# Stick-breaking weights by summation by parts: values replaced by their steps, running products used as they are

## The chip, the cores and the metric

The kernel runs on one core of a Trainium2 chip. The metric is the device time of one execution in microseconds; times below are the median of several executions, and every duration comes from one profiled execution.

## The reference, cut to what matters

The program is a trunk of two layers over 1024 tokens of width 1024. The first layer mixes tokens with two groups of attention heads, eight heads of width 64 each; the second mixes them with a recurrence; each layer ends with a feed-forward block. The change lies in the second head group of the first layer, stick-breaking attention:

```
z = einsum('bqhd,bkhd->bhqk', q_blk, k) * scale
causal = kpos[None, :] < qpos[:, None]
log_beta = log_sigmoid(z)
log_1m_beta = where(causal, log_sigmoid(-z), 0.0)
after = cumsum(log_1m_beta, axis=3, reverse=True) - log_1m_beta
w = where(causal, exp(log_beta + after), 0.0)
out = einsum('bhqk,bkhd->bqhd', w, v)
```

So for a query q the weight of key k is sigmoid(z_k) times the product of sigmoid(-z_j) over the keys j between k and q. Call C_k the product of sigmoid(-z_j) over all j from k up to the query, with C = 1 at the query and behind it. Then w_k = C_(k+1) - C_k, a difference of neighbouring running products.

## The kernel before, in words

**Tiling.** Heads are worked in pairs p. Pairs 4 to 7 are the stick-breaking heads, pairs 0 to 3 the softmax heads; the sequence is 4, 5, 6, 7, 0, 1, 2, 3. For each pair `project` makes queries and keys: four groups (queries and keys, each for two halves of the tokens) of 24 TensorE matmuls of 128x512 (lines 166 to 168) into PSUM tile `psq`, of which there are two buffers. ScalarE and VectorE take every group out of PSUM (lines 326 to 335) before its buffer can be used again. Values are made for two pairs at once by `v_tile` (lines 291 to 293) and taken out by `evacuate` (lines 303 to 306) into tiles `v`, 128 partitions by 8 token blocks by 128 columns: token 128t + p lies in partition p, block t.

**Weights.** Each weight block (128x1024 fp32, 512 KB) is loaded by a DMA that SyncE (SP) issues into a tile `raw`, of which there are three buffers, and is split into a rounded high part (`whi`, line 155, ScalarE) and the rest (`wlo`, line 156, VectorE). When both have read it, the `raw` buffer is free.

**Attention.** `attend` takes blocks of 128 queries, i = 0 to 7. For a stick-breaking head TensorE makes scores `sc` (lines 389, 390), ScalarE takes the sigmoid into `pr` (line 397), GpSimd (POOL) sets ones at and above the diagonal (line 408) and one column to the right (line 407), VectorE runs a scan from right to left (line 411) that leaves the running products C, and then subtracts neighbours (line 415) for the weights. TensorE turns 128x128 blocks of them (line 427), ScalarE copies these out of PSUM (line 431), and TensorE multiplies them with the values (line 356). Value products are held back until i = 3, 5, 6 and 7 and then run in one burst.

**What sets the order.** The program is written pair after pair, but a scheduler with a timeline of its own then orders the instructions of each engine before the program is built; it also decides which buffer a tile gets. Every engine, and the DMA queue of SyncE too, works in that order: an instruction that waits holds up all behind it on its engine. Matmuls of the next projection are thus mixed with the attention of the pair before.

Of the kernel before, what the change touches and what calls it, by code (L numbers as in the profile page):

```python
# [8 lines left out]
F32 = mybir.dt.float32  # L9
F32R = mybir.dt.float32r  # L10
BF16 = mybir.dt.bfloat16
AF = mybir.ActivationFunctionType
ALU = mybir.AluOpType
PSUM = bass.MemoryType.PSUM

P = 128
S = 1024
# [3 lines left out]
NT = S // P  # L21
# [78 lines left out]
class Trunk:  # L100
# [164 lines left out]
    def attention(self, x_src, xT_src, w_v, w_qk, bias_t, o_dst, hT, pools, open_first):  # L265
        nc, tc = self.nc, self.tc
        with ExitStack() as ctx:
# [6 lines left out]
            def turned_bank():  # L274
                return self.pt.tile([P, 512], F32, tag="tr", bufs=2, name=self.uid("tr"))
# [22 lines left out]
            def evacuate(vt, t2, both=False):  # L298
                psv = psvs.pop(t2)
                for tt in range(2):  # L300
# [4 lines left out]
                        nc.scalar.activation(vt[0][:, t, :], psv[:, tt, 0, :], AF.Copy, scale=rsc[:, t:t + 1])  # L305
                    nc.scalar.activation(vt[1][:, t, :], psv[:, tt, 1, :], AF.Copy, scale=rsc[:, t:t + 1])

            def v_alloc():
                return [ap.tile([P, NT, P], F32, tag="v", bufs=3, name=self.uid("v")) for _ in range(2)]

            def project(p, ws=(None, None)):
                st = [[ap.tile([P, S], F32R, tag="st", bufs=12, name=self.uid("st"))
                       for _ in range(3)] for _ in range(2)]
                for which in range(2):
                    w = ws[which] or self.split(w_qk[p, which], KT, P)
                    for half in range(2):
                        ps = prp.tile([P, 512], F32, tag="proj", bufs=2, name=self.uid("psq"))
                        self.proj_T(ps, w, slice(0, P), hT, half)
                        cs = slice(half * HALF, (half + 1) * HALF)
                        if which or p < 4:  # L320
                            nc.vector.tensor_tensor(ps, ps, rsb[:, cs], op=ALU.mult)
                        for h in range(2):
                            own, oth = (slice(0, 64), slice(64, P)) if h == 0 else (slice(64, P), slice(0, 64))
                            qs, k1, k2 = st[h]
                            if which == 0:
                                nc.scalar.activation(qs[own, cs], ps[own, :], AF.Copy, scale=-0.125)
                                nc.vector.scalar_tensor_tensor(
                                    qs[oth, cs], ps[own, :], -0.125, qs[own, cs].bitcast(F32),
                                    op0=ALU.mult, op1=ALU.subtract)
                            else:  # L330
                                nc.scalar.copy(k1[own, cs], ps[own, :])
                                nc.scalar.copy(k1[oth, cs], ps[own, :])
                                nc.vector.tensor_tensor(k2[own, cs], ps[own, :], k1[own, cs].bitcast(F32),
                                                        op=ALU.subtract)
                                nc.vector.tensor_copy(k2[oth, cs], k2[own, cs].bitcast(F32))
                return st

            def attend(p, st, vt):
                bias = [None, None]
# [25 lines left out]
                for i in range(NT):  # L365
                    k0 = max(0, i - 4) if p < 4 else 0
                    nb = i + 1 - k0
                    n = nb * P
# [4 lines left out]
                    w = n // n_c  # L373
                    for h in range(2):
                        qs, k1, k2 = st[h]
                        q = qs[:, i * P:(i + 1) * P]
                        if p < 4 and h == 1:
                            pr = ap.tile([P, 640], F32, tag="nata", bufs=3, name=self.uid("pr"))
                        else:
                            pr = ap.tile([P, 1024], F32, tag="nat", bufs=4, name=self.uid("pr"))  # L380
                        if p < 4:
                            mn = ap.tile([P, 2], F32, tag="mn", bufs=4, name=self.uid("mn"))
                            mn = [mn[:, c:c + 1] for c in range(n_c)]
                            sm = ap.tile([P, 1], F32, tag="sm", bufs=4, name=self.uid("sm"))
                        for c in range(n_c):
                            sc = pp.tile([P, 512], F32, tag="sc", bufs=3, name=self.uid("sc"))[:, :w]
                            ks = slice(k0 * P + c * w, k0 * P + c * w + w)
                            cs = slice(c * w, c * w + w)
                            nc.tensor.matmul(sc, q, k1[:, ks], start=True, stop=False)
                            scored = nc.tensor.matmul(sc, q, k2[:, ks], start=False, stop=True).ins  # L390
                            if p < 4:
                                off = 640 - n + c * w
                                nc.vector.tensor_tensor_reduce(
                                    pr[:, cs], sc, bias[h][:, off:off + w], 1.0, 3e38,
                                    op0=ALU.add, op1=ALU.min, accum_out=mn[c])
                            else:
                                nc.scalar.activation(pr[:, cs], sc, AF.Sigmoid, scale=rsc[:, i:i + 1])
                        if p < 4:
                            if n_c == 2:
                                nc.vector.tensor_tensor(mn[0], mn[0], mn[1], op=ALU.min)  # L400
                            nc.scalar.activation(pr[:, :n], pr[:, :n], AF.Exp, bias=mn[0], scale=-1.0,
                                                 accum_out=sm)
                            nc.vector.reciprocal(sm, sm)
                            nc.gpsimd.tensor_scalar(pr[:, :n], pr[:, :n], sm, 1.0, op0=ALU.mult, op1=ALU.mult)
                        else:
                            if n < S:
                                nc.gpsimd.memset(pr[:, n:n + 1], 1.0)
                            nc.gpsimd.affine_select(pr[:, n - P:n], pr[:, n - P:n], pattern=[[-1, P]],  # L408
                                                    compare_op=ALU.is_gt, fill=1.0, base=0,
                                                    channel_multiplier=1)  # L410
                            nc.vector.tensor_tensor_scan(  # L411
                                pr[:, 0:n][:, ::-1], pr[:, 0:n][:, ::-1], self.zero.to_broadcast([P, n]),
                                1.0, op0=ALU.mult, op1=ALU.add)
                            m = n if n < S else n - 1
                            nc.vector.tensor_tensor(pr[:, 0:m], pr[:, 1:m + 1], pr[:, 0:m], op=ALU.subtract)
                            if m < n:
                                nc.vector.memset(pr[:, m:n], 0.0)
                        nat.append(pr)
                    if p == seq[-1]:
                        self.scored.append(scored)  # L420
# [1 line left out]
                    for b0 in range(0, len(blocks), 4):  # L422
                        bl = blocks[b0:b0 + 4]
                        tr = turned_bank()
                        pt = ap.tile([P, 512], F32, tag="pt", bufs=7, name=self.uid("pt"))
                        for j, (kb, h) in enumerate(bl):
                            turned = nc.tensor.transpose(tr[:, j * P:(j + 1) * P],  # L427
                                                         nat[h][:, kb * P:(kb + 1) * P], self.ident).ins
                        w = len(bl) * P
                        if p >= 4 or (b0 // 4) % 2 == 0:  # L430
                            nc.scalar.copy(pt[:, :w], tr[:, :w])
                        else:
                            nc.vector.tensor_copy(pt[:, :w], tr[:, :w])
                        groups.append((i, nb, k0, bl, pt))
                        if not stretch:
                            values(groups, [])
                            groups = []
# [9 lines left out]
            vt = v_alloc()  # L447
# [89 lines left out]
            wk = self.split(None, KT, P, raw=wk)  # L537
            spread(1)
            st = project(seq[0], (wq, wk))
            for j, p in enumerate(seq):  # L540
                if j == 7:
                    prj.close()
                    pools[0] = open_first()
                attend(p, st, vt)
                if j < 7:
                    q = seq[j + 1]
                    if q % 2 == 0:
                        wv = v_weights(q // 2)
                        vt = v_alloc()
                        for t2 in range(4):  # L550
                            v_tile(q // 2, wv, vt, t2)
                            evacuate(vt, t2, q < 4)
                    st = project(q)


    def psum(self):
# [695 lines left out]
```

## Time and profile before

| | |
|---|---|
| time, median of 3 | 2198.3 us (2197.07 to 2202.79) |
| profiled execution, its own time | 2198.43 us |
| span from first to last instruction | 2196.6 us |
| TensorE busy | 2161.5 us, 98% |
| VectorE busy | 1540.9 us, 70% |
| ScalarE busy | 1171.1 us, 53% |
| GpSimd busy | 217.7 us, 10% |
| stick-breaking pairs 4 to 7 | from about 35 to about 303 us of the span |

Busy time of TensorE is the union of matmuls whose ends are modelled, so a share of 98% doesn't mean that no time is lost. In the rows, PE is TensorE, DVE VectorE, ACT ScalarE, POOL GpSimd and SPq the DMA queue of SyncE; L415 is line 415 of the program. Only some 270 us of the span hold what the change touches; the rest is feed-forward, recurrence and softmax attention.

### The profile page before, as it was taken

The numbers are of one execution on the slowest core, as the hardware profiler recorded it, in microseconds if no ns is written. First come the engines' busy times: TensorE is split into PE (matmuls) and PEld (weight loads), VectorE is DVE, ScalarE is ACT, GpSimd is POOL, SyncE is SP. The second block draws the span as 40 slices with busy tenths as digits, with TensorE's granted clock in tenths as the row PEclk, the third lists the DMA queues.
The fourth block names the chain that finished last, engine by engine and source line by source line (L and its number), as shares of the span: only waits on it lengthen the run. The fifth ranks groups of instructions, "written<-read, shape, count | busy, mean of one in ns | idle before, by whom it ended". The sixth has DMA issues, their size and how long they took to land.

```text
span 2196.6 us, 30590 instructions
## 1 busy us (share of the span) xinstructions
PE 2161.5 (98%) x11140; PEld 1803.2 (82%) x11140; DVE 1540.9 (70%) x2526; ACT 1171.1 (53%) x2174; POOL 217.7 (10%) x450
## 2 busy tenths in 40 slices
PE   9999999999999999999999999999999999999998
PEld 8888889878788888888887777888788888888886
DVE  5877865656878777776767677437787777758675
ACT  6655555556755444443446676528754444424443
POOL 2111113121100000000001333102000000000011
PEclk9999999999999999999999999999999999999999
DMA  7101011126323333336468411356233333328565
GB/s 273 34 30 49 27 37 49 54 84 221 137 91 111 117 98 115 94 123 230 144 183 253 130 58 39 100 192 221 86 120 106 101 112 99 115 87 287 172 182 155
DMA packets 168279, 270.21 MB, mean 123 GB/s; under 512 B 13889, under 2 KB 94785, under 8 KB 168129
## 3 DMA queue, kind: packets, MB, share of 16 engines
q1 hardware_dynamic: 167488, 266.18, 37.8%
q10 hardware_dynamic: 640, 2.10, 0.3%
q8 instruction: 87, 1.43, 0.3%
q14 instruction: 64, 0.52, 0.1%
HBM read 202.69 MB, written 65.54 MB: 122 GB/s over the span
## 4 chain that ended last, share of the span: by engine, by line
PE 87%; DVE 5%; DMA 3%; ACT 3%; issue 2%; POOL 0%; SPq 0%; POOLq 0%; ACTq 0%; DVEq 0%
PE ps L742 12%; PE ps L744 12%; PE ps L743 12%; PE ps L585 8%; PE ps L827 5%; PE ps L829 5%; PE ps L828 5%; PE tr L427 3%; PE pso L356 3%; PE psq L166 2%; PE psq L167 2%; PE psq L168 2%; PE ps L166 2%; PE ps L167 2%; PE ps L168 2%
## 5 line engine op out<-in xcount | busy, mean ns | idle before, releaser
L742 PE MATMUL ps<-hS,q 128*128 128x512 f32 (+1 forms) x1288 | 490.2, 381 | 0.7 <-ACT hS L96 0.4
L743 PE MATMUL ps<-hS,q 128*128 128x512 f32 (+1 forms) x1288 | 489.6, 380 | 0.9 <-DVE hS L89 0.9
L744 PE MATMUL ps<-hS,q 128*128 128x512 f32 (+1 forms) x1288 | 489.0, 380 | 0.0
L713 DVE TENSOR_TENSOR q<-raw,q 128x512 fp32r<-128x512 f32 x308 | 204.5, 685 | 181.6 <-ACT q L712 181.0
L743 PEld LDWEIGHTS ps<-hS,q 128*128 128x128 f32 x1288 | 242.7, 188 | 47.7 <-DVE hS L89 1.3
L742 PEld LDWEIGHTS ps<-hS,q 128*128 128x128 f32 x1288 | 242.3, 188 | 47.3 <-ACT hS L96 0.8
L744 PEld LDWEIGHTS ps<-hS,q 128*128 128x128 f32 x1288 | 242.7, 188 | 45.9
L712 ACT CAST q<-raw 128x512 fp32r<-128x512 f32 x308 | 177.7, 616 | 162.5 <-DVE raw L721 129.4
L828 PE MATMUL ps<-o,o 128*128 128x512 f32 x616 | 240.0, 390 | 0.5 <-DVE o L823 0.5
L829 PE MATMUL ps<-o,o 128*128 128x512 f32 x616 | 238.0, 390 | 0.5 <-DVE o L957 0.5
L700 ACT ACTIVATE raw<-raw,gcol 128x256 f32<-128x256 f32 x352 | 150.3, 498 | 143.3 <-DMA raw<-in_ffn_w_up_dram 71.6
L827 PE MATMUL ps<-o,o 128*128 128x512 f32 x616 | 221.4, 391 | 3.3 <-ACT o L956 3.0
L822 ACT CAST o<-raw 128x512 fp32r<-128x512 f32 x184 | 110.8, 621 | 160.3 <-PE ps L829 59.1
L182 POOL TENSOR_SCALAR rs<-ss 128x1 f32<-128x1 f32 x52 | 24.6, 473 | 1423.6 <-ACT junk L178 1356.9
L823 DVE TENSOR_TENSOR o<-raw,o 128x512 fp32r<-128x512 f32 x184 | 123.1, 686 | 56.1 <-ACT o L822 55.3
L827 PEld LDWEIGHTS ps<-o,o 128*128 128x128 f32 x616 | 115.5, 188 | 30.2 <-ACT o L956 4.8
L828 PEld LDWEIGHTS ps<-o,o 128*128 128x128 f32 x616 | 115.6, 188 | 25.3 <-DVE o L823 1.5
L829 PEld LDWEIGHTS ps<-o,o 128*128 128x128 f32 x616 | 115.6, 188 | 25.1 <-DVE o L957 1.4
L156 DVE TENSOR_TENSOR wlo<-raw,whi 128x1024 fp32r<-128x1024 f32 x76 | 93.4, 1228 | 58.5 <-ACT whi L155 57.8
L411 DVE TENSOR_TENSOR_SCAN pr<-pr,zero 128x128 f32<-128x128 f32 (+7 forms) x64 | 86.8, 1360 | 30.7 <-POOL pr L408 25.7
L155 ACT CAST whi<-raw 128x1024 fp32r<-128x1024 f32 x76 | 79.7, 1050 | 50.2 <-PE ps L167 19.9
L166 PE MATMUL psq<-hT,whi 128*128 128x512 f32 x256 | 101.8, 397 | 0.1
(206 smaller groups left out, 4314.2 us busy)
## 6 DMA issues: line engine op xcount, KB each, us to landing
raw<-in_ffn_w_gate_dram SPq DMA_DIRECT2D x44, 512.0 KB, 4.2
raw<-in_ffn_w_up_dram SPq DMA_DIRECT2D x44, 512.0 KB, 4.2
gS<-c SPq DMA_DIRECT2D x88, 256.0 KB, 3.6
raw<-gS SPq DMA_DIRECT2D x88, 256.0 KB, 2.8
gA<-c SPq DMA_DIRECT2D x66, 256.0 KB, 3.4
raw<-in_ffn_w_down_dram SPq DMA_DIRECT2D x63, 256.0 KB, 4.4
raw<-gA SPq DMA_DIRECT2D x44, 256.0 KB, 2.8
t<-in_ffn_w_down_dram SPq DMA_DIRECT2D x22, 512.0 KB, 6.8
```

Source lines behind the costliest of these rows:

```text
L166: nc.tensor.matmul(ps, wh[:, kt, cols], hh[:, kt, :], start=kt == 0, stop=False)
L585: self.matmul = nc.tensor.matmul(ps[:, n * 512:(n + 1) * 512], x, y[:, n, :], start=first and i == 0, stop=last and i == len(passes) - 1).ins
L700: nc.scalar.activation(raw[:, i], raw[:, i], AF.Copy, scale=gain[:, 4 * k + i:4 * k + i + 1])
L712: self.last = nc.scalar.copy(t[:, 0], src).ins
L713: self.last_lo = nc.vector.tensor_tensor(t[:, 1], src, t[:, 0].bitcast(F32), op=ALU.subtract).ins
L742: nc.tensor.matmul(ps, a[:, 0, kt, :], bh, start=kt == 0, stop=False)
L743: nc.tensor.matmul(ps, a[:, 0, kt, :], bl, start=False, stop=False)
L744: self.matmul = nc.tensor.matmul(ps, a[:, 1, kt, :], bh, start=False, stop=kt == 3).ins
L823: tt(t[:, 1], src, t[:, 0].bitcast(F32), op=ALU.subtract)
L827: nc.tensor.matmul(ps, a[0], b[:, 0], start=first, stop=False)
L828: nc.tensor.matmul(ps, a[0], b[:, 1], start=False, stop=False)
L829: nc.tensor.matmul(ps, a[1], b[:, 0], start=False, stop=last)
```

## The change

The sum of (C_(k+1) - C_k) v_k over the keys is rewritten by parts: it equals the sum of (1 - C_k) (v_k - v_(k-1)), with v before the first token taken as 0. So the differences move from the weights, which are made for every query, to the values, which are made once.

- The subtraction of neighbours on VectorE, the memset of one column on GpSimd and a memset on VectorE go away: `pr` keeps the running products.
- ScalarE's copy of the turned blocks out of PSUM becomes an activation that computes 1 - C.
- A new function `steps` turns the values into steps. For each of the two `v` tiles it loads a tile `prev` in one of the three `raw` buffers: partitions 1 to 127 get v of partitions 0 to 126, one DMA; partition 0 gets the last partition's row, one block further on, a second DMA; one piece is set to 0 by GpSimd. Then VectorE subtracts `prev` from `v` in place. `steps` is called after the projection of pair 4, and again after that of pair 6. The subtraction is held behind the last copy of keys of the projection before it.

```diff
+            def steps(vt):
+                for v in vt:
+                    prev = self.main.tile([P, NT, P], F32, tag="raw", bufs=3, name=self.uid("prev"))
+                    nc.sync.dma_start(prev[1:P], v[0:P - 1])
+                    nc.sync.dma_start(prev[0:1, 1:NT], v[P - 1:P, 0:NT - 1])
+                    nc.gpsimd.memset(prev[0:1, 0:1], 0.0)
+                    with self.behind([self.stacked]):
+                        nc.vector.tensor_tensor(v, v, prev, op=ALU.subtract)
...
-                                nc.vector.tensor_copy(k2[oth, cs], k2[own, cs].bitcast(F32))
+                                self.stacked = nc.vector.tensor_copy(k2[oth, cs], k2[own, cs].bitcast(F32)).ins
...
-                            if n < S:
-                                nc.gpsimd.memset(pr[:, n:n + 1], 1.0)
                             nc.gpsimd.affine_select(pr[:, n - P:n], pr[:, n - P:n], pattern=[[-1, P]],
                                                     compare_op=ALU.is_gt, fill=1.0, base=0,
                                                     channel_multiplier=1)
                             nc.vector.tensor_tensor_scan(
                                 pr[:, 0:n][:, ::-1], pr[:, 0:n][:, ::-1], self.zero.to_broadcast([P, n]),
                                 1.0, op0=ALU.mult, op1=ALU.add)
-                            m = n if n < S else n - 1
-                            nc.vector.tensor_tensor(pr[:, 0:m], pr[:, 1:m + 1], pr[:, 0:m], op=ALU.subtract)
-                            if m < n:
-                                nc.vector.memset(pr[:, m:n], 0.0)
...
-                        if p >= 4 or (b0 // 4) % 2 == 0:
+                        if p >= 4:
+                            nc.scalar.activation(pt[:, :w], tr[:, :w], AF.Copy, bias=1.0, scale=-1.0)
+                        elif (b0 // 4) % 2 == 0:
                             nc.scalar.copy(pt[:, :w], tr[:, :w])
...
             st = project(seq[0], (wq, wk))
+            steps(vt)
             for j, p in enumerate(seq):
...
                     st = project(q)
+                    if q == 6:
+                        steps(vt)
```

The scheduler orders the changed program anew. Two places matter for the prediction. The first is the DMA queue of SyncE at the start, around the loads of the weights of pair 5. In these rows `prev_659` and `prev_664` are the two shifted copies for pairs 4 and 5; `raw_1085` and then `raw_1149` are the query and key weights of pair 5 before, `raw_1063` and `raw_1127` the same two after; the `raw` tiles from `in_attn_w_v_dram` are the value weights of pairs 6 and 7. Brackets give the semaphores that an issue waits for: DMAHW0 to DMAHW7 are those of the transfers, taken in turn, so that the row with DMAHW6 first is the transfer that sets DMAHW6. Before:

```order
L453 DMA x_483<-in_x_dram 128x1024 [waits DMAHW3_49,DVE_49]
L137 DMA raw_1085<-in_attn_w_qk_dram 128x1024 [waits DMAHW4_49,DVE_49]
L453 DMA x_487<-in_x_dram 128x1024 [waits DMAHW5_49,DVE_49]
L453 DMA x_489<-in_x_dram 128x1024 [waits DMAHW6_49,DVE_49]
L344 DMA bias_3369<-in_bias_t_dram 128x640 [waits DMAHW7_49]
L344 DMA bias_3374<-in_bias_t_dram 128x640 [waits DMAHW0_49]
L344 DMA bias_3907<-in_bias_t_dram 128x640 [waits DMAHW1_49]
L344 DMA bias_3912<-in_bias_t_dram 128x640 [waits DMAHW2_49]
L137 DMA raw_1149<-in_attn_w_qk_dram 128x1024 [waits DMAHW3_49,DVE_49]
L137 DMA raw_1643<-in_attn_w_v_dram 128x1024 [waits DMAHW4_49,DVE_49]
L137 DMA raw_1649<-in_attn_w_v_dram 128x1024 [waits DMAHW5_49,DVE_49]
```

And after the change:

```order
L353 DMA bias_3804<-in_bias_t_dram 128x640 [waits DMAHW1_49]
L312 DMA prev_659<-v_115 1x16x56 [waits DMAHW2_49,Activation_49]
L311 DMA prev_659<-v_115 127x1024 [waits DMAHW3_49,Activation_49]
L311 DMA prev_664<-v_116 127x1024 [waits DMAHW4_49,DVE_49,Activation_49]
L312 DMA prev_664<-v_116 1x16x56 [waits DMAHW5_49]
L137 DMA raw_1063<-in_attn_w_qk_dram 128x1024 [waits DMAHW6_49,DVE_49]
L137 DMA raw_1127<-in_attn_w_qk_dram 128x1024 [waits DMAHW7_49,DMAHW6_49,DVE_49]
L137 DMA raw_1589<-in_attn_w_v_dram 128x1024 [waits DMAHW7_49,DMAHW0_49,DVE_49]
L137 DMA raw_1595<-in_attn_w_v_dram 128x1024 [waits DMAHW1_49,DMAHW0_49,DVE_49]
```

The first weight load of pair 5 stood ahead of the last two blocks of x; now it stands behind the four new transfers. The next three loads also wait for the semaphore of the load just ahead of them and for VectorE: they take its buffer, one after another, while the two `prev` tiles hold the other two.

The second place is ScalarE's queue at the same time, while the queries (`psq_533`, `psq_562`) and keys (`psq_591`, `psq_625`) of pair 4 are taken out of PSUM. Before:

```order
L326 ACTIVATE st_530<-psq_533 64x512
L155 CAST whi_1645<-raw_1643 128x1024
L326 ACTIVATE st_527<-psq_562 64x512
L326 ACTIVATE st_530<-psq_562 64x512
L331 CAST st_528<-psq_591 64x512
L332 CAST st_528<-psq_591 64x512
L331 CAST st_531<-psq_591 64x512
L332 CAST st_531<-psq_591 64x512
L155 CAST whi_1651<-raw_1649 128x1024
```

And after the change:

```order
L335 ACTIVATE st_530<-psq_533 64x512
L155 CAST whi_1065<-raw_1063 128x1024
L335 ACTIVATE st_527<-psq_562 64x512
L335 ACTIVATE st_530<-psq_562 64x512
L155 CAST whi_1129<-raw_1127 128x1024
L340 CAST st_528<-psq_591 64x512
L341 CAST st_528<-psq_591 64x512
L155 CAST whi_1591<-raw_1589 128x1024
L340 CAST st_531<-psq_591 64x512
L341 CAST st_531<-psq_591 64x512
```

The casts of the four blocks that are loaded behind the copies (the fourth, `whi_1597<-raw_1595`, stands a few rows on) now stand between the instructions that free the PSUM buffers of pair 4's projection. At the second call the picture is the same: the query weights of pair 7 (`raw_2363`) stand right behind the new transfers on SyncE,

```order
L312 DMA prev_1959<-v_1601 1x16x56 [waits DVE_49,Activation_49,Pool_49]
L311 DMA prev_1959<-v_1601 127x1024 [waits Activation_49]
L311 DMA prev_1964<-v_1602 127x1024 [waits DMAHW2_49,DVE_49,Activation_49]
L312 DMA prev_1964<-v_1602 1x16x56
L137 DMA raw_2363<-in_attn_w_qk_dram 128x1024 [waits DMAHW3_49,DVE_49]
L137 DMA raw_2427<-in_attn_w_qk_dram 128x1024 [waits DMAHW4_49,DMAHW3_49,DVE_49]
```

where before that load (`raw_2439`) stood behind weight loads only, ahead of the first output store of pair 4. On ScalarE the cast of `raw_2363` comes after the last sigmoid of pair 5 and ahead of the first evacuation of pair 6's queries.

## The prediction, made before the changed kernel had run

> **What bounds the kernel now.** I read the page first, then TensorE's waits while pairs 4 to 7 run, then the busy time by stretches.
>
> ```profile
> span 2196.6 us, 30590 instructions
> PE 2161.5 (98%) x11140; PEld 1803.2 (82%) x11140; DVE 1540.9 (70%) x2526; ACT 1171.1 (53%) x2174; POOL 217.7 (10%) x450
> ```
>
> TensorE bounds the kernel, at 98%. So time taken from VectorE is worth something only where TensorE waits for VectorE. The waits of TensorE from 40 to 300 us, the stick-breaking stage (engine, who waits for whom: total, times, longest):
>
> ```profile
> PE tr L427 <- DVE pr L415: 3.1, 3, 1.1
> PE psv L291 <- DVE st L333: 1.5, 1, 1.5
> PE sc L389 <- ACT pr L397: 0.2, 1, 0.2
> ```
>
> The subtraction that goes away (L415) releases 3.1 us of waits; 1.5 us more is a PSUM buffer that a loaded VectorE freed late. By stretches of 20 us, TensorE falls short of 20.00 in four, where pair 5 and pair 6 run out of projection matmuls (columns: busy of PE, PEld, DVE, ACT, POOL, then clock, DMA share, GB/s):
>
> ```profile
> 100.00:120.00 20.00, 18.30 (x181) 16.46 (x179) 13.51 (x17) 10.23 (x22) 2.56 (x11) 1.00 0.01 2
> 120.00:140.00 20.00, 19.00 (x187) 18.16 (x186) 16.20 (x19) 11.95 (x30) 3.78 (x15) 1.00 0.04 14
> 220.00:240.00 20.00, 18.95 (x187) 17.39 (x185) 15.39 (x17) 8.35 (x17) 3.75 (x7) 1.00 0.00 1
> 240.00:260.00 20.00, 18.89 (x180) 17.32 (x178) 17.20 (x23) 12.43 (x29) 4.89 (x20) 1.00 0.04 14
> ```
>
> Their idle time is 1.70 + 1.00 + 1.05 + 1.11 = 4.9 us. That is what a lighter VectorE can win; the rest of the stage is TensorE's own work.
>
> **The change: what goes and what is cheap.** On VectorE and GpSimd, by groups from 40 to 300 us (count, busy us, mean ns, idle before):
>
> ```profile
> L415 DVE TENSOR_TENSOR pr<-pr 128x128 f32<-128x128 f32 (+7 forms) x64 | 48.0, 754 | 1.5
> L407 POOL MEMSET pr<- 128x1 f32 x55 | 5.2, 98 | 81.4 <-PE tr L427 79.7 <-DVE pr L411 1.3
> L156 DVE TENSOR_TENSOR wlo<-raw,whi 128x1024 fp32r<-128x1024 f32 x14 | 17.1, 1219 | 6.8 <-ACT whi L155 6.6
> ```
>
> VectorE loses 48.0 us. It gains four subtractions of 128x1024, 4 x 1.22 = 4.9 us by the third row, an operation of the same kind and size. GpSimd loses 5.2 us that nobody waits for. Most of this hides behind TensorE: I take a **gain of 4 us**, of 4.9 at most visible, and 0 at least.
>
> ScalarE's 64 copies of 128x512 become activations with a constant scale and bias. Rows for both kinds from PSUM, 40 to 305 us:
>
> ```profile
> L431 ACT COPY pt<-tr 128x512 f32<-128x512 f32 x64 | 36.5, 591 | 29.4 <-PE tr L427 29.1
> L326 ACT ACTIVATE st<-psq 64x512 fp32r<-64x512 f32 x20 | 11.8, 592 | 17.8 <-DVE st L327 16.1 <-DVE psq L321 1.4 <-PE psq L168 0.3
> ```
>
> 591 against 592 ns: nothing. The added bias has no row; ScalarE's 53% would hide some ns each. GpSimd's four small memsets take the place of 55: nothing.
>
> **The copies.** The expensive part may be the shifted copies of 127 rows. Two facts come from the listing of the order. The one-row copies stand there as 1x16x56: the row was cut into 16 pieces, the number of DMA engines. The 127-row copies stand uncut, and 127 is a prime: no equal shares but one or 127. Every other large transfer has 128 rows (or 64), 8 to an engine. What a 127-row copy costs is then bounded by two readings: dealt out like a 128-row load, or carried by one engine. These rows price them: a lone weight load between 42 and 50 us (size, time to landing), its packets (count, MB, share of 16 engines' 8 us), and the stretch 4 to 16 us, in which loads fill the DMA engines.
>
> ```profile
> raw<-in_attn_w_qk_dram SPq DMA_DIRECT2D x1, 512.0 KB, 3.6
> q1 hardware_dynamic: 144, 0.52, 24.0%
> 4.00:16.00 12.00, 9.89 (x58) 8.63 (x57) 9.64 (x21) 10.58 (x24) 0.00 (x0) 0.86 1.02 409
> ```
>
> Dealt out: 3.6 us, issue to landing. On one engine: 409 GB/s over 16 is 25.6 GB/s each, and 127 x 4096 B = 520 KB take **20.3 us**; at the pace of the lone load (0.52 MB in 24.0% of 16 x 8 us = 30.7 us, 17 GB/s, most of it first latency) 30.5 us. I take one engine, since the uncut row has no other equal share, and 20.3 us, since 127 packets in a row are nearer to the filled stretch.
>
> The Trainium skill states it as a rule ("DMA: Bandwidth & Descriptors", section "Why a DMA increments its semaphore by 16 and not by 1"): a transfer uses the largest number of engines up to 16 that divides the slowest dimension of both sides, and it names 127 partitions as a case that gets one. By this rule the sum is the one below; by the nearest row, 3.6 us, it would be the first rival's. No run here shows it yet.
>
> **Who waits for the copies.** A transfer lands behind what its queue already holds:
>
> ```profile
> small<-in_g0col_dram SPq DMA_DIRECT2D x1, 4.0 KB, 1.6
> gcol<-in_gcol_dram SPq DMA_DIRECT2D x1, 12.0 KB, 10.4
> ```
>
> 12 KB issued behind loads took 10.4 us; 4 KB issued first took 1.6. A weight load has a sixteenth of its rows on the engine that carries the copies, so it lands only when both copies are through: 2 x 20.3 = 40.6 us late. The rows for the first call (start, duration): the last value written, the cast that follows, the last evacuation of the first query group, VectorE's part of the queries, the fourth projection group of pair 4 on TensorE (two matmuls, 0.22 us apart), the last evacuation of its keys on ScalarE and on VectorE, the first burst of value products:
>
> ```profile
> 40.72 0.36 ACT L306 ACTIVATE v<-psv,small 128x128 f32<-128x128 f32 x1
> 40.97 1.04 ACT L155 CAST whi<-raw 128x1024 fp32r<-128x1024 f32 x1
> 44.05 0.59 ACT L326 ACTIVATE st<-psq 64x512 fp32r<-64x512 f32 x1 [0.94 <-DVE st L327]
> 50.14 0.69 DVE L327 SCALAR_TENSOR_TENSOR st<-psq,st 64x512 fp32r<-64x512 f32 x1
> 53.22 0.39 PE L166 MATMUL psq<-hT,whi 128*128 128x512 f32 x1
> 53.44 0.39 PE L167 MATMUL psq<-hT,whi 128*128 128x512 f32 x1
> 63.80 0.58 ACT L332 CAST st<-psq 64x512 fp32r<-64x512 f32 x1
> 65.64 0.42 DVE L335 CAST st<-st 64x512 fp32r<-64x512 f32 x1
> 87.17 0.55 PE L356 MATMUL pso<-pt,v 128*64 128x128 f32 x6
> ```
>
> The copies can start at 41.1; `raw_1063`, issued right behind, lands at 41.1 + 40.6 + 3.6 = 85.3. ScalarE meets its cast (formerly at 40.97) between the evacuations of `psq_533` and `psq_562` and waits from about 44.6. TensorE does the third group, then has no PSUM buffer: the fourth needs `psq_562` out. After 85.3 come, in order, the cast 1.04, VectorE's split 1.22, its half of the queries 0.69, ScalarE's 0.59 and VectorE's 0.69 again, 4.2 us: 89.5. TensorE stands from 53.2 to 89.5, 36.3 us. Then three more weights pass one buffer, each 3.6 landing + 1.04 cast + 1.22 split = 5.9 us, and ScalarE's queue has the keys' evacuations between their casts: the casts end at 86.3, 92.2, 98.1 and 104.0, the last keys at 105.2 instead of 64.4. **First call: +41 us.** VectorE's stepping, behind that, waits for nothing more; the first value burst stood at 87.2, so its own lateness is covered.
>
> Second call, the same rows: last value, last sigmoid of pair 5 before, third group of pair 6's projection, last evacuation.
>
> ```profile
> 148.27 0.42 ACT L306 ACTIVATE v<-psv,small 128x128 f32<-128x128 f32 x1
> 160.07 0.69 ACT L397 ACTIVATE pr<-sc,small 128x512 f32<-128x512 f32 x1
> 162.99 0.39 PE L166 MATMUL psq<-hT,whi 128*128 128x512 f32 x1
> 183.44 0.58 ACT L332 CAST st<-psq 64x512 fp32r<-64x512 f32 x1
> ```
>
> In the times of before, `raw_2363` lands at 148.7 + 40.6 + 3.6 = 192.9. ScalarE meets its cast after that sigmoid, near 160, with pair 6's first query evacuation behind it. The third group, at 163.0, needs that buffer: 192.9 + 4.2 = 197.1, 34 us late. Three more casts at 5.9 us: the last keys leave at 211.6 + 4 x 0.58 = 213.9 instead of 184.0, 30 us late. I take **+32 us**.
>
> A long stand also costs clock. After TensorE's gaps at 445 to 455 us:
>
> ```profile
> 450.00:455.00 5.00, 3.31 (x33) 2.81 (x28) 4.84 (x18) 3.31 (x7) 1.25 (x2) 1.00 0.99 362
> 455.00:460.00 5.00, 5.00 (x21) 4.29 (x20) 2.09 (x10) 2.77 (x9) 2.46 (x5) 0.66 0.34 127
> ```
>
> The clock was 0.66 over the 5 us behind: 1.7 us lost. Two stands: **+3 us**.
>
> **Sum**, on the profiled execution's own 2198.4 us (span 2196.6; the median of the runs is 2198.3): + 41 + 32 + 3 - 4 = +72, so **2270 us**. With copies of 30.5 us it is 4 x 10.2 = 41 more, 2311; with the second stand at 30 and one group of overlap at each call (24 matmuls at 0.23 us, 5.5 us), 2257. Its own range is 2257 to 2311.
>
> **Rivals.** *The copies are dealt out.* One mechanism: 127 rows shared over 16 engines, 8 or fewer each, land in 3.6 us, and the next weight 1.3 us behind that. `raw_1063` lands at 41.1 + 3.6 + 2 x 1.3 = 47.3 and its cast, 3 us late, is done before TensorE asks for the buffer at 53.2; at the second call 155 comes before 160. So nothing is lost, and the 4 us are won: **2194 us**, from 2187 to 2200, not slower. It decides as long as both copies together stay under some 6 us. For it: all other loads land so. Against it: the uncut 127.
>
> *The loads pass the copies.* If a weight's share on the busy engine isn't held up, casts come in time and only VectorE's stepping waits. It stands ahead of the scans; at the first call the keys are out at 66.1 (64.4 and VectorE's part) and the second copy lands at 83, 17 us; at the second call 191 against 184, 7 us: 2198.4 + 24 - 4 = **2218 us**. For it: nothing but that the data needn't wait; against it: the 10.4 us of gcol.
>
> *One engine is slower still.* If a lone engine moves 4 KB in over 0.24 us, as the lone load's 30.7 us / 144 = 0.21 us almost does, copies take over 30.5 us: **2330 us** at 35 us each, by 4 x 14.7 = 59 more than 2270.
>
> **How the numbers follow.** One engine with the queue behind it 0.70, dealt out 0.14, passing 0.10, slower still 0.06. The likeliest gives 2270. The range for 8 in 10 runs from 2215, which takes in the passing case, to 2312, the upper bound of the copy; dealt out and slower still are left out. Faster or slower here means by over 0.3%, 6.6 us, about what a measurement of this kernel can tell from no change. Dealt out gives 2194, within that; I give 0.06 to faster and 0.08 to the same, and the rest, 0.86, is slower.
>
> **What would show it.** In the changed profile: the 127-row issues landing after 20 us or more, the second of a pair after 40; a DMA share near one sixteenth, 0.06, at 25 GB/s, from about 42 to 84 us; ScalarE's line 155 waiting for DMA `raw` by some 40 and 33 us; TensorE near idle from 53 to 89 us with a half clock behind. Line 315 at 1.2 us, line 434 at 0.59 us and no waits of line 430 for VectorE's old line 415 would show the cheap terms. Copies landing in 4 us would make the prediction wrong at its base; waits on line 315 with line 155 in time would show the second rival.

## The result, and the profile after

| | before | after |
|---|---|---|
| time, median of 4 | 2198.64 us (2197.07 to 2202.79) | 2267.28 us (2266.48 to 2269.19) |
| profiled execution: span | 2196.6 us | 2265.7 us |
| TensorE busy | 2161.5 us | 2168.4 us |
| TensorE idle (span less busy) | 35.1 us | 97.3 us |

The changed kernel takes 1.0315 times as long, with a 95% interval of 1.0302 to 1.0328. The forecast was 2270 us, in a range from 2215 to 2312. In the profile the span grew by 69.1 us: 62.2 us of them are idle time of TensorE and 6.9 us are busy time of the same 11140 matmuls, which means that some of them ran slower.

The page of the changed kernel: the span, the busy time by engine, and TensorE's granted clock in 40 slices.

```profile
span 2265.7 us, 30452 instructions
PE 2168.4 (96%) x11140; PEld 1809.5 (80%) x11140; DVE 1499.8 (66%) x2458; ACT 1170.5 (52%) x2174; POOL 217.6 (10%) x398
PEclk9697999999999999999999999999999999999999
```

VectorE has 41.1 us less work (1540.9 less 1499.8), and the kernel became slower all the same. The clock is low in the second and the fourth slice of 57 us, in which TensorE stands behind the two calls of `steps`. TensorE's waits from 40 to 345 us (engine, who waits for whom: total, times, longest):

```profile
PE psq L166 <- DVE st L336: 33.6, 1, 33.6
PE tr L430 <- ACT pt L434: 32.7, 2, 32.1
PE sc L398 <- ACT st L341: 1.7, 1, 1.7
```

Two stands make up nearly all of it. The engines named here are not the cause; they wait in their turn. ScalarE's own waits in the same stretch lead one step back, to the load of a weight:

```profile
ACT whi L155 <- DMA raw<-in_attn_w_qk_dram: 81.3, 4, 38.8
```

And SyncE's queue shows what was ahead of that load (timeline of SyncE's issues, 36 to 70 us: start, duration):

```profile
36.27 0.64 SPq L312 DMA_DIRECT2D prev<-v  x1
37.42 9.07 SPq L311 DMA_DIRECT2D prev<-v  x2
46.54 20.02 SPq L312 DMA_DIRECT2D prev<-v  x1
66.66 0.53 SPq L137 DMA_DIRECT2D raw<-in_attn_w_qk_dram  x1
```

The weight of pair 5 is issued at 66.66 us, behind the four transfers of `steps`. What the DMA engines did in the 20 us from 44 to 64 (packets, MB, mean rate and packet sizes; then queue, packets, MB, share of 16 engines):

```profile
DMA packets 127, 0.52 MB, mean 26 GB/s; under 512 B 1, under 2 KB 1, under 8 KB 127
q1 hardware_dynamic: 127, 0.52, 6.4%
```

One hundred and twenty-seven packets of 4 KB in 20 us are 0.16 us for each, one after another, and 6.4% is about one sixteenth: as much as one DMA engine at work while fifteen stand. A copy of 127 rows therefore takes 127 x 0.16 = 20.3 us.

The weight that is issued at 66.66 us shows the same from the other side. From 67.5 to 70 us the DMA engines moved 220 GB/s, most of its 512 KB, and then 26 GB/s again until about 81 us; its cast starts at 82.10. So nearly all of the load moved while the second copy was still going on, and a last share of it waited for the engine that carried the copy.

The other end of the chain is the stretch in which TensorE resumes. First ScalarE's casts of the four weights and the last keys of pair 4, then TensorE's last matmul ahead of the stand and the first ones behind it (timeline: start, duration, and in brackets the idle time and what ended it):

```profile
82.10 1.04 ACT L155 CAST whi<-raw 128x1024 fp32r<-128x1024 f32 x1 [38.76 <-DMA raw<-in_attn_w_qk_dram]
87.93 1.04 ACT L155 CAST whi<-raw 128x1024 fp32r<-128x1024 f32 x1 [2.19 <-DMA raw<-in_attn_w_qk_dram]
93.90 1.05 ACT L155 CAST whi<-raw 128x1024 fp32r<-128x1024 f32 x1 [1.73 <-DMA raw<-in_attn_w_v_dram]
99.73 1.05 ACT L155 CAST whi<-raw 128x1024 fp32r<-128x1024 f32 x1 [0.41 <-DMA raw<-in_attn_w_v_dram]
101.40 0.58 ACT L341 CAST st<-psq 64x512 fp32r<-64x512 f32 x1
```

```profile
52.64 0.39 PE L168 MATMUL psq<-hT,wlo 128*128 128x512 f32 x1
86.61 0.77 PE L166 MATMUL psq<-hT,whi 128*128 128x512 f32 x1 [33.58 <-DVE st L336]
87.17 0.63 PE L167 MATMUL psq<-hT,whi 128*128 128x512 f32 x1
87.60 0.63 PE L168 MATMUL psq<-hT,wlo 128*128 128x512 f32 x1
```

The casts follow one another by 5.8 to 6.0 us: that is the chain through a single `raw` buffer. The matmuls behind the stand follow by 0.56 and 0.43 us; before the change, in the same group, by 0.22 us. The busy time by stretches says over how long that lasts (busy time of PE, PEld, DVE, ACT, POOL; then clock, DMA share, GB/s):

```profile
64.00:84.00 20.00, 0.00 (x0) 0.00 (x0) 0.83 (x1) 1.63 (x2) 0.00 (x0) 0.50 0.14 47
84.00:90.00 6.00, 3.39 (x8) 2.77 (x9) 2.77 (x4) 1.64 (x2) 0.00 (x0) 0.50 0.29 87
90.00:110.00 20.00, 18.09 (x75) 14.62 (x75) 15.42 (x22) 11.14 (x18) 4.01 (x6) 0.90 0.33 106
200.00:230.00 30.00, 0.00 (x0) 0.00 (x0) 0.00 (x0) 0.17 (x1) 0.00 (x0) 0.56 0.12 41
230.00:240.00 10.00, 7.37 (x25) 5.42 (x25) 4.51 (x5) 5.85 (x10) 0.00 (x0) 0.62 0.26 61
```

From these rows the work lost to the clock is about 3.39 x 0.50 + 18.09 x 0.10 + 7.37 x 0.38 = 6.3 us, close to the 6.9 us by which TensorE's busy time grew. In the stage alone (from 40 to 305 us before, from 40 to 375 us after) it grew from 260.1 to 266.4 us, by the same 6.3 us. In the rows from 64 to 84 and from 200 to 230 hardly any engine works: the core waits for one DMA engine, and from about 81 us on for the chain behind it.

### The profile page after: what moved, and what is told of

Read it like the earlier page. It is cut to its first block, busy times and chain, and to the rows that moved or that the text cites. A ratio compares the mean times of both kernels' runs of the same rounds, so it can differ in the third digit from the quotient of the medians.

```text
span 2265.7 us, 30452 instructions
## 1 busy us (share of the span) xinstructions
PE 2168.4 (96%) x11140; PEld 1809.5 (80%) x11140; DVE 1499.8 (66%) x2458; ACT 1170.5 (52%) x2174; POOL 217.6 (10%) x398
## 4 chain that ended last, share of the span: by engine, by line
PE 86%; DMA 4%; DVE 3%; ACT 3%; SPq 2%; issue 1%; POOL 0%; POOLq 0%; ACTq 0%; DVEq 0%
PE ps L750 12%; PE ps L751 12%; PE ps L752 12%; PE ps L593 8%; PE ps L837 5%; PE ps L836 5%; PE ps L835 5%; PE tr L430 3%; PE pso L365 3%; PE psq L166 2%; PE psq L168 2%; PE psq L167 2%; PE ps L167 2%; PE ps L166 2%; PE ps L168 2%; SPq L312 2%
## 5 line engine op out<-in xcount | busy, mean ns | idle before, releaser
L166 PE MATMUL psq<-hT,whi 128*128 128x512 f32 x256 | 105.0, 410 | 33.8 <-DVE st L336 33.6
```

The source lines that it names most:

```text
L166: nc.tensor.matmul(ps, wh[:, kt, cols], hh[:, kt, :], start=kt == 0, stop=False)
```

## The experiments

All experiments edit the changed kernel, except `copies_only`, which edits the kernel before. A time without a count of runs comes from one execution.

The first question is whether the loss hangs on the number of rows in one transfer, on the bytes, or on the arithmetic.

**Two transfers that divide by 16 and by 15** (`spread`). 127 rows become 112 and 15.

```diff
-                    nc.sync.dma_start(prev[1:P], v[0:P - 1])
+                    nc.sync.dma_start(prev[1:113], v[0:112])
+                    nc.sync.dma_start(prev[113:P], v[112:P - 1])
```

> Theory (a 127-row copy rides on one DMA engine, 20.3 us each, and holds up the weights behind it): 112 rows can be dealt out 7 to each of 16 engines and the other 15 rows one to each of 15, so both parts together land in some 4 us; the weights come in time, no stand of TensorE over 3 us, and the lighter VectorE wins some 4 us: 2194 us, 2187 to 2200. Rival (the weights' place behind the copies and their passing through one buffer cost the time, whatever a copy takes): the order of the loads is the same here, so it stays at 2250 to 2268 us.

Measured: 2194.78 us (2192.93 to 2198.28, 10 runs) against 2197.44 us before, ratio 0.9987 [0.9978, 0.9997]. The loss is gone, with the same bytes through the same queue. DMA issues of this kernel between 36 and 60 us (count, size, median time to landing):

```profile
prev<-v SPq DMA_DIRECT2D x2, 448.0 KB, 4.1
prev<-v SPq DMA_DIRECT2D x2, 60.0 KB, 3.6
raw<-in_attn_w_qk_dram SPq DMA_DIRECT2D x2, 512.0 KB, 4.0
```

448 KB land in 4.1 us, where 508 KB took 20.3, and the weight behind them lands in 4.0 us. From 38.4 to 42 us, with the copies alone in flight, the DMA share is 0.86 at 242 GB/s: nearly all engines work. The same stretches whose idle time was to be won (columns as above):

```profile
100.00:120.00 20.00, 20.00 (x197) 18.67 (x195) 9.36 (x6) 9.88 (x21) 1.48 (x5) 1.00 0.01 2
120.00:140.00 20.00, 19.82 (x191) 18.53 (x191) 11.84 (x10) 13.60 (x34) 4.22 (x10) 1.00 0.04 14
220.00:240.00 20.00, 19.76 (x200) 18.50 (x200) 9.34 (x10) 8.72 (x19) 1.89 (x6) 1.00 0.06 22
240.00:260.00 20.00, 20.00 (x191) 18.95 (x188) 12.66 (x14) 12.61 (x28) 3.60 (x9) 1.00 0.08 28
```

TensorE falls short by 0.4 us here, where it was 4.9 before. So the lighter VectorE does win what the change could win in these stretches. By the ratio it wins 2.9 us net, between 0.7 and 4.8 by its interval.

**One row more** (`rows113`). The same program with 113 and 14 rows in place of 112 and 15; the order on every engine is the same.

```diff
-                    nc.sync.dma_start(prev[1:113], v[0:112])
-                    nc.sync.dma_start(prev[113:P], v[112:P - 1])
+                    nc.sync.dma_start(prev[1:114], v[0:113])
+                    nc.sync.dma_start(prev[114:P], v[113:P - 1])
```

> The dealt-out kernel with one row moved from the second part of each copy to the first: 113 and 14 rows in place of 112 and 15; every engine's order is the same. Theory (a row count without a common share goes to one engine): 113 is a prime, so 113 x 0.16 = 18.1 us a copy on one engine, 2.2 us less than 127 rows, and the two stands are back: 2267 - 2 x 2 x 2.2 = 2258 us, 2250 to 2268. Rival (the length of the transfer, the shift by one partition or the kind of copy is what made it slow, not the count of rows): 2195 us as with 112 and 15.

Measured: 2258.88 us against 2198.53 us before, 60.4 us more, where `spread` was 2.7 us less. Waits of TensorE from 40 to 345 us:

```profile
PE psq L166 <- DVE st L337: 29.8, 1, 29.8
PE tr L431 <- ACT pt L435: 28.7, 2, 28.1
```

This is the sharpest of the runs. One row moved from one transfer to the other, in each copy, costs 63 us, and both stands are back, shorter by 3.8 and 4.0 us than those of the changed kernel. Two copies of 113 rows are 28 packets of 0.16 us fewer than two of 127, that is 4.5 us. Bytes, order and arithmetic are the same, so it is the number of rows and how it divides.

**Only the copies** (`copies_only`). The kernel before, with `steps` called at the same two places; its subtraction writes into `prev`, which nobody reads, and the weights are still made by subtraction.

```diff
+            def steps(vt):
+                for v in vt:
...
+                        nc.vector.tensor_tensor(prev, v, prev, op=ALU.subtract)
...
+            steps(vt)
...
+                    if q == 6:
+                        steps(vt)
```

> The kernel before with the shifted copies and their subtraction added (its result goes to the copy's own tile and is not used), the weights made by subtraction as before. Theory: the copies alone do the harm, 2198.6 + 41 + 32 = 2272 us, about 4 above the changed kernel. Rival (the activation 1 - C or the missing subtraction, through the new order, is part of the loss): clearly below, 2210 to 2255 us.

Measured: 2271.34 us, 4.1 us above the changed kernel. Waits of TensorE from 40 to 345 us:

```profile
PE psq L166 <- DVE st L336: 34.5, 2, 34.0
PE psq L166 <- DVE pr L426: 32.5, 1, 32.5
```

The copies, with their buffers and their subtraction, make the whole loss, and the rest of the change takes a little off it.

**Half the width** (`half_width`). The copies take four of eight token blocks; the rest of `prev` is set to 0, so the steps of the last 512 tokens are left out.

```diff
-                    nc.sync.dma_start(prev[1:P], v[0:P - 1])
-                    nc.sync.dma_start(prev[0:1, 1:NT], v[P - 1:P, 0:NT - 1])
+                    nc.sync.dma_start(prev[1:P, 0:NT // 2], v[0:P - 1, 0:NT // 2])
+                    nc.gpsimd.memset(prev[:, NT // 2:NT], 0.0)
+                    nc.sync.dma_start(prev[0:1, 1:NT // 2], v[P - 1:P, 0:NT // 2 - 1])
```

> Half of the columns (four of eight token blocks) are copied, the rest of the tile is set to 0 by GpSimd, so the steps of the last 512 tokens are left out. Theory: still 127 rows on one engine, but 2 KB each, about 10.3 us a copy by bytes; each of the two stands gets 20 us shorter, 2267 - 40 = 2227 us. If one engine's price were by row and not by byte, 2267 stays. Rival (order and buffers alone): 2260 or more.

Measured: 2210.23 us, 17 us under the expectation. Waits of TensorE from 40 to 345 us, and packets of 2 KB in the 8 us from 36 to 44:

```profile
PE psq L166 <- DVE st L337: 12.2, 1, 12.2
PE tr L431 <- ACT pt L435: 3.8, 1, 3.8
```

```profile
DMA packets 96, 0.19 MB, mean 24 GB/s; under 512 B 1, under 2 KB 1, under 8 KB 96
```

96 packets in 8 us are 0.083 us each, half of 0.16: the rate of one engine holds, and a copy takes 10.6 us. What I had left out is when the copies start. Timeline of SyncE's issues in this kernel, first and second call, and the second call in the changed kernel:

```profile
28.27 6.02 SPq L311 DMA_DIRECT2D prev<-v  x2
136.48 1.35 SPq L311 DMA_DIRECT2D prev<-v  x2
```

```profile
185.08 9.49 SPq L311 DMA_DIRECT2D prev<-v  x2
```

Half a copy needs only the values of token blocks 0 to 3. At the first call it starts 9.1 us earlier than in the changed kernel (28.27 against 37.42). At the second call the changed kernel writes its last value of blocks 0 to 3 at 161.71 us and of blocks 4 to 7 at 184.81 us, and its copies wait for the latter; the half copies don't, so the weight behind them comes while pair 5 still has attention to run, and that stand nearly vanishes. The run confirms the rate of one engine and not the sum that was expected, since its edit moved two things.

**Weights ahead of the copies** (`whole_nat`). The 127-row copies stay whole, but `prev` comes from another pool (tag `nat`, four buffers), so that the weights keep three `raw` buffers; those of pair 5 then stand ahead of the copies in SyncE's queue.

```diff
-                    prev = self.main.tile([P, NT, P], F32, tag="raw", bufs=3, name=self.uid("prev"))
+                    prev = ap.tile([P, 1024], F32, tag="nat", bufs=4, name=self.uid("prev")).rearrange("p (a b) -> p a b", a=NT)
```

> The copies of 127 rows as they are, in an attention buffer, so that the weights of pair 5 stand ahead of them and keep three buffers. Theory with the queue as the way in which the copies do harm: most of the loss goes, and what is left is that VectorE meets the second stepping some 16 us early at the first call and 20 at the second, TensorE stands some 12 and 15 us: 2193 + 28 + 3 = 2224 us, 2208 to 2242. Rival A (nothing but late weights cost): 2193 to 2197 us. Rival B (the busy engine slows everything, whatever stands behind it): 2255 us or more.

Measured: 2238.01 us, 14 us above the value expected and inside its span. Waits of TensorE from 40 to 345 us, and the second subtraction of each call in the timeline of VectorE (start, duration, idle time ahead and what ended it):

```profile
PE tr L430 <- DVE pr L418: 18.8, 1, 18.8
PE sc L398 <- ACT pr L406: 15.9, 2, 15.7
```

```profile
85.93 1.23 DVE L315 TENSOR_TENSOR v<-v,prev 128x1024 f32<-128x1024 f32 x1 [18.32 <-DMA prev<-v]
223.55 1.23 DVE L315 TENSOR_TENSOR v<-v,prev 128x1024 f32<-128x1024 f32 x1 [19.84 <-DMA prev<-v]
```

The weights come in time now: in this stage no cast of line 155 waits for a load, and about 30 us are won back. The two stands together are 34.7 us where 28 were expected, and TensorE's busy time is 6.2 us above that of the kernel before (2167.7 against 2161.5) where 3 were expected; that is most of the 14 us. But VectorE works in order too: the subtraction of `steps` waits for its copy, and the scans behind it wait with it. TensorE stands for 18.8 and 15.9 us. So slow copies cost about 45 us here (2238 against 2193 for the quick ones in the same pool, `spread_nat` below) even when no engine waits for a load behind them in the DMA queue.

**Both repairs together** (`spread_nat`). The pool of `whole_nat` with the 112 and 15 rows of `spread`.

> The copies dealt out as 112 and 15 rows, and into a buffer of the attention rows (four buffers of 128x1024) in place of a weight buffer, so that weights keep three buffers and stand ahead of the copies at the first call. Theory: 2194 us like the other dealt-out form, at most 3 us less, since no weight waits there either. Rival (the one weight buffer has a price of its own, up to 3 x 5.9 us a call): 5 to 15 us below the dealt-out form in the weight buffers.

Measured: 2192.89 us (2189.61 to 2197.71, 10 runs), ratio 0.9981 [0.9971, 0.9990] to the kernel before. It has the lowest time of the versions that compute all of the reference, by the ratio 4.2 us under the kernel before, and 74 us under the changed one. In its profile from 40 to 345 us TensorE waits once:

```profile
PE sc L399 <- ACT pr L407: 0.2, 1, 0.2
```

Against `spread`, which still shows one wait of 2.2 us there, it is 1.9 us better; the two intervals overlap, so that part isn't settled.

**Another queue** (`pool_queue`). The uncut copies of 127 rows, issued by GpSimd instead of SyncE.

```diff
-                    nc.sync.dma_start(prev[1:P], v[0:P - 1])
-                    nc.sync.dma_start(prev[0:1, 1:NT], v[P - 1:P, 0:NT - 1])
+                    nc.gpsimd.dma_start(prev[1:P], v[0:P - 1])
+                    nc.gpsimd.dma_start(prev[0:1, 1:NT], v[P - 1:P, 0:NT - 1])
```

> The copies as they are, 127 rows into weight buffers, but issued from GpSimd, whose queue is not that of the weights. Theory if the shares are made alike there (one engine): weights pass, their loads through one buffer stay, and VectorE's stepping waits 17 and 7 us: 2218 us, 2205 to 2235. If GpSimd's queue deals 127 rows out over 16 engines: 2195 us, 2190 to 2202. Rival (it is the engine, whichever queue feeds it, that holds the weights): 2255 to 2270 us.

Measured: 2194.73 us. The row of GpSimd's queue from 30 to 110 us (packets, MB, share), and its issues of the copy there (count, size, median time to landing):

```profile
q0 software_dynamic: 352, 1.05, 5.4%
```

```profile
prev<-v POOLq DMA_DIRECT2D x2, 508.0 KB, 4.9
```

The same 127 rows land in 4.9 us. That is 106 GB/s, four times the 26 GB/s of one engine: GpSimd's queue does deal them out. It isn't 127 rows as such that cost 20 us, then, but 127 rows through SyncE's queue. The Trainium skill has this exception ("DMA: Bandwidth & Descriptors", section "Why a DMA increments its semaphore by 16 and not by 1"): on trn2 GpSimd's path spreads some direct copies over all 16 engines, with 127 partitions among its examples. The 4.9 us agree with it.

**No copy at all** (`no_copy`). The copies are replaced by a memset of `prev` on GpSimd, so the values aren't turned into steps.

```diff
-                    nc.sync.dma_start(prev[1:P], v[0:P - 1])
-                    nc.sync.dma_start(prev[0:1, 1:NT], v[P - 1:P, 0:NT - 1])
-                    nc.gpsimd.memset(prev[0:1, 0:1], 0.0)
+                    nc.gpsimd.memset(prev, 0.0)
```

> No shifted copies: the tile is set to 0 by GpSimd, so the values are not turned into steps (that part of the computation is left out); all else is as in the changed kernel. Theory: the rest of the change is worth 3 to 5 us, no more, since TensorE bounds the stage: 2194 us, 2190 to 2197, and not below the dealt-out kernels by more than 2. Rival (the 48 us taken from VectorE are worth much more once the copies are out): 2170 to 2188 us.

Measured: 2194.62 us (2191.14 to 2198.71, 9 runs) against 2198.53 us before, ratio 0.9979 [0.9969, 0.9990], 4.6 us less. This is what the rewritten arithmetic is worth when its data comes free. A better way of shifting the values has little more to win, as far as this order of instructions goes: `spread_nat` is already there within the intervals.

## Why the prediction was right, step by step

**One DMA engine carries a copy, 20.3 us.** Right, in its sign and its size: 127 packets in 20 us, 6.4% of 16 engines. The bound of 3.6 us was the price for rows that divide (4.1 us for 112 in `spread`); the bound of 30.5 us, from a lone load's pace, was too careful, since the packets do follow one another without that load's first latency. `rows113` shows that the step rests on the number of rows.

The Trainium skill's rule that was weighed in the prediction ("DMA: Bandwidth & Descriptors", section "Why a DMA increments its semaphore by 16 and not by 1"), the largest number of engines up to 16 that divides the slowest dimension, agrees with every run for SyncE's queue: 127 and 113 rows move at 26 GB/s, the pace of one engine, and 112 rows are dealt out. For GpSimd's queue it doesn't hold, as `pool_queue` shows.

**The weight behind the copies lands late and its cast stands in ScalarE's queue.** Right: ScalarE waits 38.8 us for that load, and 39.1 us in `copies_only`, which has the whole loss. The moments were 3 us off. The copies were to begin at 41.1 and the cast at 85.3; they began at 37.4 and 82.1. I had taken the time of the last value from the kernel before, 40.72 us; in the new order it is written at 37.29.

**First call, +41 us.** Over by some 6 us. Of it, 36.3 us were the stand of TensorE (33.6 measured) and the rest was the delay of the keys by the single buffer. The chain through that buffer is as predicted, 5.8 to 6.0 us for each weight where 5.9 was said, and the last keys leave at 102.0 us instead of 64.4, 37.6 late. But only 1.7 us of waiting (line 398) come from the keys: once TensorE had a PSUM buffer again, it had other matmuls to run while the keys came. A late operand was counted in full where part of it was covered.

**Second call, +32 us.** 32.7 us in the waits. The reason is the same, but it isn't the instruction I named: not a projection of pair 6 without a PSUM buffer (line 166), but a turned block of pair 5 (line 430), because the copies of `pt` out of PSUM stand behind the same cast on ScalarE. In `copies_only` it is line 166 that waits, for 32.5 us. Which one hits the blocked engine first depends on the order; the length of the stand is about the same in these two, 32.1 and 32.5 us. The moments were right too. The last value is written at 184.81 us and the cast starts at 229.83; less the 36.5 us by which the first call has set everything back, these are 148.3 and 193.3, where 148.27 and 192.9 were counted with.

**Clock, +3 us.** Under by about 4 us: TensorE's busy time grew by 6.9 us. I had taken one slow stretch of 5 us for each stand, from short gaps elsewhere in the kernel. Behind these stands of over 30 us, the granted clock was 0.50 up to 90 us, 0.90 over the next 20 us, and 0.62 from 230 to 240 us.

**The gain, 4 us.** Right, within 0 to 4.9. The waits of TensorE before, 4.8 us, are down to 0.4 us of the same short kind in the changed profile, and `spread`, `spread_nat` and `no_copy` win 2.9, 4.2 and 4.6 us. VectorE's 41 us less are worth no more, since TensorE sets the end.

**The cheap terms.** The four subtractions, and the turned blocks on ScalarE by shape, in the groups of the changed kernel from 40 to 345 us (count, busy us, mean ns, idle before):

```profile
L315 DVE TENSOR_TENSOR v<-v,prev 128x1024 f32<-128x1024 f32 x4 | 4.8, 1245 | 0.1
L434 ACT ACTIVATE pt<-tr 128x512 f32<-128x512 f32 x57 | 33.3, 602 | 18.2 <-PE tr L430 18.0
```

4.8 us where 4.9 was said. The activation with scale and bias takes 602 ns where the copy took 591, 11 ns more each; that is 0.6 us in all on an engine that is busy for half the span. Nothing, as said.

**The sum.** By the waits and the busy time: 33.6 + 32.7 + 1.7 of stands, + 6.9 of clock, - 4.4 of short waits make 70.5 us, where the span grew by 69.1. The forecast was +72. It had some 6 us too much for the first call and 4 us too little for the clock, and these partly cancelled: that much of the closeness of 2270 to 2267.28 is luck.

**The rivals.** The copies dealt out (2194): not through SyncE's queue, but `spread` and `pool_queue` show what it would have been, 2195, so that its arithmetic was sound. Loads that pass the copies (2218): fell. In the trace the load isn't even issued until 66.66 us, and then it lands 15 us later, with the end of the second copy. But its price was also too low: `whole_nat` makes weights come ahead of the copies and still takes 2238, because at the second call VectorE waits 19.84 us for the second copy, where I had 7; at the first call its 18.32 us are near my 17. A still slower engine (2330): fell, by 0.16 us for 4 KB.

## What to carry to other kernels

Count the rows of a transfer, not only its bytes: here 127 or 113 rows through SyncE's queue cost 18 to 20 us a copy where 112 rows with nearly the same bytes cost 4, and a split into 112 + 15 took all of it back. A slow transfer is paid for by whatever stands behind it in an in-order queue, first the next load, then the engine that meets its data, then the engine that needs a buffer from that one; follow that chain before taking a copy for free. And relief for an engine that isn't the bound is worth only the bound's waits for it: 41 us less work on VectorE were worth 3 to 5 us.

## What the runs showed of the hardware that I had not expected

- **The issuing engine itself is held.** SyncE spent 9.07 us on its two 127-row issues and then 20.02 us on a transfer of 3.5 KB behind them, where an issue elsewhere in that queue takes 0.53 or 0.64 us. At the second call the same short transfer takes 20.04 us, though in the order it waits for no semaphore. I had thought of late landings alone. No row says what holds SyncE. Here it can have changed little, because the last share of the load behind had to wait for the busy engine anyway.
- **The same copy is quick or slow by the queue that issues it:** 4.9 us from GpSimd against 20.3 us from SyncE, for 127 rows.
- **A stand of TensorE costs more than its length.** Two stands of 33.6 and 32.1 us brought 6.9 us of slower matmuls behind them, about a tenth on top. The price doesn't follow the length: in `whole_nat` two stands of half that length, 18.8 and 15.7 us, go with 6.2 us, and the clock behind them is down to 0.50 as well. In the four runs without a wait of over 3 us TensorE is busy for 2159.5 to 2161.5 us, in the four with stands of over 15 us for 2165.5 to 2168.4 us.
